# Moving sums of weights between three stages of a hybrid transformer block on one core

## The chip, the cores and the metric

The kernel runs on one core of one Trainium2 chip. The metric is the device time of one execution in microseconds (us). Three runs of the kernel before took 3123.35, 3115.73 and 3134.21 us, median 3123.35 us. Names of engines: PE is TensorE, PEld its weight loads, DVE is VectorE, ACT is ScalarE, POOL is GpSimd, SP is SyncE, which here issues nearly all DMAs.

## What is computed

One layer over 2064 tokens (16 learned meta tokens and 2048 inputs) with 1024 features. An input projection feeds three mixers (a linear recurrence, an attention with forgetting, and a delta-rule recurrence), an output projection joins them, and a feed-forward block follows:

```python
h = concat([meta, x])
p = rms_norm(h, g_mix_pre) @ w_in            # 1024 -> 3080 columns, three groups
mixed = concat([rg_lru(p), fox_attention(p), rwkv7(p)]) @ w_out
h = h + rms_norm(mixed, g_mix_post)
f = causal_dwconv3(rms_norm(h, g_ffn_pre) @ ffn_up)   # 1024 -> 2 * 2816
gate, val = split(f)
f = (gelu(gate) * val) @ ffn_down            # 2816 -> 1024
out = (h + rms_norm(f, g_ffn_post))[16:]
```

All numbers are float32. Every large product is made of three matmuls on operands that are split into a high part and the rest (`mm3`, lines 148 to 152). The split is a copy on ACT (L1528, rounded to the matmul's format) and a subtraction (L1529) on DVE or POOL.

## The kernel before

**Stages.** The input projection runs in three parts over the tokens (`w_in_part`), one unit for each 128 columns of `w_in`; each unit loads 512 KB of weights (`raw`, L143), splits them (L144, L145) and multiplies. From the first part on, the recurrences are woven in between its units. Then come the attention, the output projection, the first feed-forward product (`ffn_up`), and the second (`Down`).

**Seven products for eight.** Both feed-forward products are blocked two by two and use seven products, so some operands are sums of blocks of weights. For the first weights and a column block j of 128, the four raw blocks are `g0`, `g1` (gate, upper and lower half of the rows) and `v0`, `v1` (value); the sums are `s1 = v0 + v1`, `s2 = s1 - g0`, `s4 = g1 - s2`, `s3 = g0 - v0`, each 128x512 numbers. For the second weights, a pair k of row blocks gives four sums `t1` to `t4` in the same way, also 128x512 each.

**`ffn_up`.** There are 66 units: three blocks of tokens (`sup` 0 to 2), in each 22 column blocks j. A unit is seven products of 12 matmuls. While a unit's products run, the next unit's seven weight operands are made by an `UpWeights` object: a raw tile `uq` is loaded (L1587) into a ring of 10 buffers (`RAWS`), and split into a tile `uw` of a ring of 10. In block 0 of tokens every unit is "own": its four raw blocks are loaded, POOL computes the four sums (L1601), SP stores them to the scratch `scr_us` (L1602). In blocks 1 and 2 the unit is not own: it loads three raw blocks and four kept sums, seven loads. `POOLED` says which of the seven operands' subtractions L1529 run on POOL and not on DVE: one (operand 6) in an own unit, two (3 and 6) in another. At its end each unit multiplies gate and value on POOL (L1646, twice) and stores the result (L1647).

**`between`.** Between the units of a block, the next block's tokens are normalised and transposed (`ffn_norm`, L1489 and L1490) and their sums made on POOL (L1523).

**`weight_sums`.** The sums of the second weights, for ten pairs k: a load of 1 MB (L1550), four POOL operations (L1547), a store of 1 MB to `scr_ds` (L1559), through one tile `ds`. The code asks for them beside the units of parts 1 and 2 of the input projection. A scheduler at build time sets the order of each engine's instructions, and nothing ties these to a place: it puts them in the first part, at 25 to 195 us.

Each engine, and SP's queue of DMA issues, runs its instructions in the order of the program, so one that waits holds those behind it.

Of the kernel before, what the change touches and what calls it, by code (L numbers as in the profile page):

```python
# [8 lines left out]
F32 = mybir.dt.float32  # L9
# [4 lines left out]
ALU = mybir.AluOpType  # L14
# [4 lines left out]
P = 128  # L19
# [9 lines left out]
FF = 2816  # L29
NFF = FF // P  # L30


class Core:


    def __init__(self, tc, ctx):
        self.tc = tc
        self.nc = tc.nc
        self.ctx = ctx
        self.uid = 0  # L40
# [98 lines left out]
def load_parts(core, raws, src, hi, lo):  # L139

    pool, tag, bufs = raws
    raw = pool.tile(list(hi.shape), F32, tag=tag, name=core.n("raw"), bufs=bufs)
    core.nc.sync.dma_start(raw[:], src)  # L143
    core.nc.scalar.activation(hi, raw[:], AF.Copy)  # L144
    core.nc.vector.tensor_tensor(lo, raw[:], hi, op=ALU.subtract)  # L145

# [247 lines left out]
class Attn:  # L394
# [1071 lines left out]
HK = KD // 2  # L1466
# [74 lines left out]
SUMS = ("s2", "s4", "s3", "s1")  # L1541


def weight_sums(core, pool, w_down, scr):

    nc = core.nc
    sub = lambda o, x, y: nc.gpsimd.tensor_tensor(o, x, y, op=ALU.subtract)  # L1547
    for k in range(DOWN_PAIRS):
        t = pool.tile([P, 4, 512], F32, tag="us", name=core.n("ds"))
        nc.sync.dma_start(  # L1550
            t[:].rearrange("p (i h) c -> p i (h c)", h=2),
            w_down[2 * P * k : 2 * P * (k + 1), :].rearrange("(i p) c -> p i c", p=P),
        )
        l0, r0, l1, r1 = (t[:, i] for i in range(4))
        sub(l0, r0, l0)
        sub(r0, r1, r0)
        sub(r1, r1, l0)
        sub(l1, l1, r1)
        nc.sync.dma_start(scr["ds"][k], t[:].rearrange("p s c -> p (s c)"))  # L1559
        yield  # L1560

# [6 lines left out]
class UpWeights:  # L1568
# [2 lines left out]

    def __init__(self, core, raws, ring, w_up, scr, j, sup):
        self.core, self.raws, self.ring, self.w_up, self.scr, self.j = core, raws, ring, w_up, scr, j
        self.own = sup == 0
        self.raw = {s: self.load(s) for s in ("g0", "v0", "v1", "g1")} if self.own else {}

    def new(self):
# [30 lines left out]
        return t  # L1608

POOLED = (3, 6), (6,)

# [277 lines left out]
def hybrid_block_kernel(ctx: ExitStack, tc: tile.TileContext, args, out):  # L1891
    a = {s: v[0] if s != "meta_tokens" else v for s, v in args.items()}
    nc = tc.nc
    core = Core(tc, ctx)
    scr = scratch(tc, ctx, core)
    x, meta = a["x"], a["meta_tokens"]
# [20 lines left out]
    with ExitStack() as p1:  # L1917
        core.const = pool(p1, "const1", 1)
        dp = pool(p1, "dp", 2, space=DRAM)
        rec = ExitStack()  # L1920
        ps_rw = pool(rec, "ps_rw", 2, space=PSUM, **right)
        ps_ae = pool(rec, "ps_ae", 1, space=PSUM, **right)
        gp = pool(rec, "gp", 1, **right)
        rp = pool(rec, "rp", 1, **right)
        with ExitStack() as p1a:
            ps_mm = pool(p1a, "ps_mm", 5, space=PSUM)
            g_pre = spread(pool(p1a, "gpre", 1), a["norm_mix_pre"], "g_pre")
            pools = {"xn": pool(p1a, "xn", 1), "nt": pool(p1a, "nt", 4), "w": pool(p1a, "w", 2), "st": pool(p1a, "st", 2)}
            sums = weight_sums(core, pool(p1a, "us", 1), a["ffn_down"], scr)
            following = w_in_norm(core, pools, ps_mm, x, meta, g_pre, 0)  # L1930
            for part in range(3):
                blocks = following
                if part == 0:
                    zeros = pools["st"].tile([P, PAD], F32, tag="sth", name="zeros")
                    nc.vector.memset(zeros[:], 0.0)
                    for r in range(0, A_ROWS + C_ROWS, P):
                        nc.gpsimd.dma_start(scr["p"][r : r + P, 0:PAD], zeros[:])
                units = w_in_part(core, pools, ps_mm, a["w_in"], blocks, scr)
                for _ in range(READY if part == 0 else 0):
                    next(units)  # L1940
                if part == 0:
# [28 lines left out]
        beside.finish()  # L1970
        for _ in R.ending:
            pass
        rec.close()
        p2 = ExitStack()
        ps_wo = [pool(p2, "ps_wo", 2, space=PSUM, **right)]
        with ExitStack() as p1b:
            more = pool(p1b, "ps_more", 1, space=PSUM, **right, **early)
            at = Attn(core, pool(p1b, "ap", 2, **early), pool(p1b, "ps_at", 1, space=PSUM), more, scr)
            at.run()
    qp = pool(ctx, "qp", 1, **early)  # L1980
    with ExitStack() as p3:
# [3 lines left out]
        tmp = pool(p3, "tmp", RAWS, **early)  # L1985
# [8 lines left out]
        with p2:  # L1994
# [7 lines left out]
            for i, (f, rows) in enumerate(FFN_TILES):  # L2002
# [5 lines left out]
                if i >= LATE and todo:  # L2008
                    q, f, rows = todo.pop(0)
# [8 lines left out]
        sums, ws, down = [iter(())], [], []  # L2018

        def between(sup, j):  # L2020

            sup += 1
            if j == 1 and sup < SUPERS:
                quarters[sup] = ffn_quarters(core, qp, sup)
                todo[:] = tiles[sup]
            elif j == 1:
                kept = qp.tile([P, DOWN_KEPT, 2, 512], F32R, tag="q", name=core.n("qd"))
                down.extend(kept[:, i] for i in range(DOWN_KEPT))
            elif sup == SUPERS:
                if j == DOWN_FROM:  # L2030
                    raw = lambda: tmp.tile([P, 512], F32, tag="uq", name=core.n("raw"))[:]
                    ws.append(down_operands(core, raw, lambda: down.pop(0), a["ffn_down"], scr, 0))
            elif todo:
                q, f, rows = todo.pop(0)
                ffn_norm(core, np_, ps_n, scr, f, rows, rs[q], g_fpre, quarters[sup], sup)
                if not todo:
                    sums.append(ffn_sums(core, quarters[sup], lambda: tc.issue_after(core.pooled.ins)))
            else:
                for _ in range(2):
                    next(sums[-1], None)  # L2040

        ffn_up(
            core, tmp, uw, up, ps_f, a["ffn_up"], cw, scr, between,
            lambda sup, i: ffn_operand(core, xo, quarters[sup], i),
        )
# [73 lines left out]
```

## Time and profile before

| what | value |
|---|---|
| median of three runs | 3123.35 us |
| the profiled execution's own time | 3122.89 us |
| its span | 3121.2 us |
| granted TensorE clock, mean of the span | 0.962 |
| busy: PE, PEld, DVE, ACT, POOL | 2925.9, 2492.2, 2251.1, 1452.4, 1301.9 us |
| moved by DMA | 443.72 MB, mean 142 GB/s |
| POOL, sums of the second weights (L1547) | 40 instructions, 58.3 us |
| POOL, sums of the first weights (L1601) | 88 instructions, 128.3 us |

A group's row reads: line, engine, operation, out<-in, shapes, count, then busy time, mean ns of one, and the idle time of the engine ahead of it with what ended it. "psu" are the accumulators of the first feed-forward product, "psp" those of the input projection, "rwraw" and "rwitmp" tiles of the recurrences.

### The profile page before, as it was taken

To read this page: it belongs to the slowest core of one execution; us is meant where nothing else is said; L and a number is where in the kernel's file an instruction comes from. 1 tells how busy PE (TensorE), PEld (TensorE's weight loads), DVE (VectorE), ACT (ScalarE), POOL (GpSimd) and SP (SyncE) were. 2 spreads that over 40 slices of the span, in tenths; PEclk is the share of its full clock that TensorE was granted. 3 is DMA by queue.
4 is the path that set the end of the run, shared out by engine and by line. 5 is a ranking of instruction groups with operands and counts; after the bars stand their busy time and mean duration, and the time that the engine had idled before them with its cause. 6 is when DMAs were issued, how large, how long until landed. Compare 5 with 4: busy or idle time off the path is not lost. (4 is left out here: it accounts for less than half of the span.)

```text
span 3121.2 us, 52484 instructions
## 1 busy us (share of the span) xinstructions
PE 2925.9 (94%) x18488; PEld 2492.2 (80%) x18488; DVE 2251.1 (72%) x4585; ACT 1452.4 (47%) x2716; POOL 1301.9 (42%) x1436
## 2 busy tenths in 40 slices
PE   6988999999978999999998899999999999999998
PEld 6987998999855664665576899899999999787776
DVE  6247655676688778877758898888778787547777
ACT  4135334344544444445533555566666665324332
POOL 3310001101134365446733568743533334547665
PEclk9999999999988788999999899999999999999999
DMA  6664333353353235544236555565665565535454
GB/s 205 226 204 137 101 97 100 107 140 104 97 143 81 64 84 142 130 117 107 65 107 201 162 171 158 167 193 170 166 166 166 166 188 162 174 105 167 143 161 142
DMA packets 456503, 443.72 MB, mean 142 GB/s; under 512 B 82496, under 2 KB 373514, under 8 KB 453408
## 3 DMA queue, kind: packets, MB, share of 16 engines
q1 hardware_dynamic: 455856, 439.99, 48.3%
q8 instruction: 145, 2.38, 0.3%
q14 instruction: 118, 0.97, 0.1%
q0 software_dynamic: 384, 0.39, 0.0%
HBM read 314.39 MB, written 125.87 MB: 141 GB/s over the span
## 5 line engine op out<-in xcount | busy, mean ns | idle before, releaser
L150 PE MATMUL psu<-xo,uw 128*128 128x344 f32 x1848 | 594.9, 326 | 25.2 <-DVE vb L1684 10.4
L151 PE MATMUL psu<-xo,uw 128*128 128x344 f32 x1848 | 597.1, 323 | 0.7 <-DVE xo L1529 0.7
L152 PE MATMUL psu<-xo,uw 128*128 128x344 f32 x1848 | 586.5, 322 | 0.0
L150 PE MATMUL psp<-xh,wh 128*128 128x384 f32 (+2 forms) x1152 | 382.0, 332 | 0.0
L152 PE MATMUL psp<-xh,wl 128*128 128x384 f32 (+2 forms) x1152 | 379.1, 330 | 3.0 <-DVE wl L145 3.0
L151 PE MATMUL psp<-xl,wh 128*128 128x384 f32 (+2 forms) x1152 | 378.2, 328 | 0.0
L150 PEld LDWEIGHTS psu<-xo,uw 128*128 128x128 f32 x1848 | 350.3, 190 | 31.4 <-DVE vb L1684 12.4
L1529 DVE TENSOR_TENSOR uw<-uq,uw 128x512 fp32r<-128x512 f32 x352 | 327.5, 935 | 59.5 <-ACT uw L1528 55.8
L151 PEld LDWEIGHTS psu<-xo,uw 128*128 128x128 f32 x1848 | 351.7, 190 | 1.1 <-DVE xo L1529 1.1
L152 PEld LDWEIGHTS psu<-xo,uw 128*128 128x128 f32 x1848 | 350.0, 190 | 0.0
L1528 ACT ACTIVATE uw<-uq 128x512 fp32r<-128x512 f32 x462 | 286.9, 627 | 102.8 <-PE psu L152 48.8
L640 ACT ACTIVATE p<-sc,bias 128x512 f32<-128x512 f32 (+4 forms) x352 | 197.6, 590 | 217.3 <-PE sc L636 181.8
L1640 DVE SCALAR_TENSOR_TENSOR uy<-psu,ffn_cols,uy 128x342 f32<-128x342 f32 (+1 forms) x396 | 224.0, 567 | 72.0 <-ACT uy L1638 70.9
L679 POOL TENSOR_TENSOR acc<-acc,p 128x512 f32<-128x512 f32 (+3 forms) x208 | 230.5, 1111 | 78.7 <-DVE acc L679 37.9
L1646 POOL TENSOR_TENSOR uy<-uy,uy 128x342 f32<-128x342 f32 (+1 forms) x132 | 146.3, 1109 | 224.5 <-DVE uy L1640 79.2
L152 PEld LDWEIGHTS psp<-xh,wl 128*128 128x128 f32 x1152 | 220.1, 191 | 10.3 <-issue 5.5
L150 PEld LDWEIGHTS psp<-xh,wh 128*128 128x128 f32 x1152 | 219.9, 191 | 7.1 <-issue 4.7
L151 PEld LDWEIGHTS psp<-xl,wh 128*128 128x128 f32 x1152 | 220.0, 191 | 6.4 <-issue 4.1
L1529 POOL TENSOR_TENSOR uw<-uq,uw 128x512 fp32r<-128x512 f32 x110 | 155.9, 1417 | 164.2 <-ACT uw L1528 137.8
L512 DVE TENSOR_REDUCE mc<-mx 128x1 f32<-128x400 f32 (+5 forms) x320 | 171.5, 554 | 55.3 <-PE mx L509 53.9
L1529 DVE TENSOR_TENSOR fo<-u,fo 128x896 fp32r<-128x896 f32 x88 | 104.4, 1187 | 118.6 <-ACT fo L1528 118.6
L1528 ACT ACTIVATE fo<-u 128x896 fp32r<-128x896 f32 x88 | 81.0, 922 | 230.9 <-POOL u L1756 120.9
(451 smaller groups left out, 6612.6 us busy)
## 6 DMA issues: line engine op xcount, KB each, us to landing
uq<-in_ffn_up_dram SPq DMA_DIRECT2D x220, 256.0 KB
uq<-scr_us SPq DMA_DIRECT2D x176, 256.0 KB
raw<-in_w_in_dram SPq DMA_DIRECT2D x72, 512.0 KB
scr_us<-uq SPq DMA_DIRECT2D x88, 256.0 KB
u<-scr_ff SPq DMA_DIRECT2D x88, 256.0 KB
scr_ff<-uy SPq DMA_DIRECT2D x110, 171.0 KB
q<-scr_qh SPq DMA_DIRECT2D x96, 128.0 KB
ds<-in_ffn_down_dram SPq DMA_DIRECT2D x10, 1024.0 KB
```

Source lines behind the costliest of these rows:

```text
L150: nc.tensor.matmul(out, ah, bh, start=first, stop=False, skip_group_check=more)
L151: nc.tensor.matmul(out, ah, bl, start=False, stop=False, skip_group_check=more)
L152: nc.tensor.matmul(out, al, bh, start=False, stop=last, skip_group_check=more)
L512: self.reduced = nc.vector.tensor_reduce(mc[:rows, i, ci : ci + 1], ps[:rows, :full], axis=AX.X, op=ALU.max)
L640: last = nc.scalar.activation(p[:rows, :w], ps[:rows, :w], AF.Exp, bias=bias[:rows, j : j + 1])
L679: eng.tensor_tensor(a, ps_[0][0][:rows, c0:n] if start and i == 1 else a, p[:rows, : n - c0], op=ALU.add)
L1528: core.nc.scalar.activation(hi, src, AF.Copy)
L1529: (eng or core.nc.vector).tensor_tensor(lo, src, hi, op=ALU.subtract)
L1640: stt(y[:, :n], src[:, i : n + i], cw[:, 44 * i + cc : 44 * i + cc + 1], y[:, :n], op0=ALU.mult, op1=ALU.add)
L1646: core.pooled = nc.gpsimd.tensor_tensor(v[:, :n], g[:, :n], v[:, :n], op=ALU.mult)
```

## The change

Three places get the sums. `weight_sums` goes. `up_sums` makes the sums of the first weights for the eleven odd column blocks (`EARLY`) beside the units of parts 1 and 2 of the input projection, one block after every fourth unit, through the tile that held `ds`. Its instructions on SP are ordered behind the latest load of `raw` by `issue_after`, which adds an order edge to a named instruction on the same engine. In block 0 of tokens the odd units are then no longer own: they load three raw blocks and four kept sums, and have two subtractions on POOL. The even units compute beside use as before. `down_sums` makes the sums of the second weights in blocks 1 and 2 of `ffn_up`: 40 POOL operations, one per unit and two after every fourth, each ordered behind the latest end of a unit (`core.pooled`), with four buffers of the ring of `uq` for each of ten pairs.

```diff
+def up_sums(core, pool, w_up, scr, js):
+    tt = nc.gpsimd.tensor_tensor
+    for j in js:
+        t = pool.tile([P, 4, HK, P], F32, tag="us", name=core.n("us"))
+        for u in range(2):
+            c0 = FF * u + P * j
+            nc.sync.dma_start(
+                t[:, 2 * u : 2 * u + 2].rearrange("p h k c -> p (h k) c"),
+                w_up[:, c0 : c0 + P].rearrange("(k p) c -> p k c", p=P),
+            )
+        g0, g1, v0, v1 = (t[:, i] for i in range(4))
+        tt(v1, v0, v1, op=ALU.add)
+        for o, x, y in ((v0, g0, v0), (g0, v1, g0), (g1, g1, g0)):
+            tt(o, x, y, op=ALU.subtract)
+        nc.sync.dma_start(scr["us"][j], t[:].rearrange("p s k c -> p (s k c)"))
+        yield
+def down_sums(core, raws, w_down, scr, after):
     for k in range(DOWN_PAIRS):
+        l0, r0, l1, r1 = q = [raws.tile([P, 512], F32, tag="uq", name=core.n("ds")) for _ in range(4)]
+        for i, t in enumerate(q):
+            at = P * (2 * k + i // 2)
+            nc.sync.dma_start(t[:], w_down[at : at + P, 512 * (i % 2) : 512 * (i % 2) + 512])
+        for i, (o, x, y) in enumerate(((l0, r0, l0), (r0, r1, r0), (r1, r1, l0), (l1, l1, r1))):
+            with after():
+                nc.gpsimd.tensor_tensor(o[:], x[:], y[:], op=ALU.subtract)
+            yield
+        for i, t in enumerate(q):
+            nc.sync.dma_start(scr["ds"][k, :, 512 * i : 512 * i + 512], t[:])
...
-        self.own = sup == 0
+        self.own = sup == 0 and j not in EARLY
...
+EARLY = range(1, NFF, 2)
...
-                    if part and i % 3:
-                        next(sums, None)
+                    if part and i % 4 == 0:
+                        with tc.issue_after(core.loaded.ins):
+                            next(sums, None)
...
+            for _ in range(1 + (j % 4 == 3) if sup else 0):
+                next(later, None)
```

The scheduler's order shows where this lands. First SP's queue in the first part of the input projection; `raw` are weights of `w_in`, `stp` results on their way to the scratch, `rwraw` the recurrences' reads of that scratch. Before:

```order
L1550 DMA ds_4076<-in_ffn_down_dram 128x2x1024
L209 DMA scr_p<-stp_798 128x400
L209 DMA scr_p<-stp_826 128x384
L143 DMA raw_1289<-in_w_in_dram 128x8x128
L209 DMA scr_p<-stp_860 128x400
L1559 DMA scr_ds<-ds_4076 128x2048
L209 DMA scr_p<-stp_888 128x384
L1550 DMA ds_4375<-in_ffn_down_dram 128x2x1024
L143 DMA raw_1384<-in_w_in_dram 128x8x128
```

The same place of the changed kernel:

```order
L209 DMA scr_p<-stp_798 128x400
L209 DMA scr_p<-stp_826 128x384
L143 DMA raw_1289<-in_w_in_dram 128x8x128
L209 DMA scr_p<-stp_860 128x400
L209 DMA scr_p<-stp_888 128x384
L143 DMA raw_1384<-in_w_in_dram 128x8x128
```

The loads and stores of `ds` are gone from between the loads of `raw`; the rest stands in the same order.

Second, POOL at the start of part 1, between two chains of a recurrence (`rwitmp`, L1101, which alternates with DVE). Before:

```order
L1101 TENSOR_TENSOR rwitmp_1972<-rwix_1969,rwia_1941 128x120
L1101 TENSOR_TENSOR rwitmp_1972<-rwix_1969,rwia_1941 128x128
L983 TENSOR_SCALAR rwe_2230<-rwe_2230 128x512
L1101 TENSOR_TENSOR rwitmp_2515<-rwix_2512,rwia_2484 128x16
L1101 TENSOR_TENSOR rwitmp_2515<-rwix_2512,rwia_2484 128x24
```

And in the changed kernel:

```order
L1101 TENSOR_TENSOR rwitmp_1972<-rwix_1969,rwia_1941 128x128
L983 TENSOR_SCALAR rwe_2230<-rwe_2230 128x512
L1557 TENSOR_TENSOR us_3520<-us_3520 128x512
L1559 TENSOR_TENSOR us_3520<-us_3520 128x512 x3
L1557 TENSOR_TENSOR us_4049<-us_4049 128x512
L1559 TENSOR_TENSOR us_4049<-us_4049 128x512 x3
L1101 TENSOR_TENSOR rwitmp_2515<-rwix_2512,rwia_2484 128x16
L1101 TENSOR_TENSOR rwitmp_2515<-rwix_2512,rwia_2484 128x24
```

Eight operations on `us`, which wait for loads, now stand ahead of the second chain; the tiles `us_5449` and `us_7812` are further ones right ahead of such a chain or inside it.

Third, POOL in block 0 of tokens of `ffn_up`; `uq` sums, `uy` ends of units, `q` sums of tokens, `uw` subtractions. Two units before:

```order
L1601 TENSOR_TENSOR uq_20229<-uq_20192,uq_20194 128x512
L1601 TENSOR_TENSOR uq_20192<-uq_20190,uq_20192 128x512
L1646 TENSOR_TENSOR uy_19979<-uy_19956,uy_19979 128x342
L1601 TENSOR_TENSOR uq_20249<-uq_20229,uq_20190 128x512
L1601 TENSOR_TENSOR uq_20269<-uq_20196,uq_20249 128x512
L1646 TENSOR_TENSOR uy_20022<-uy_20000,uy_20022 128x342
L1523 TENSOR_TENSOR q_18029<-q_18029 128x344 x2
L1529 TENSOR_TENSOR uw_20179<-uq_20034,uw_20179 128x512
L1601 TENSOR_TENSOR uq_20389<-uq_20352,uq_20354 128x512
L1601 TENSOR_TENSOR uq_20352<-uq_20350,uq_20352 128x512
L1646 TENSOR_TENSOR uy_20139<-uy_20116,uy_20139 128x342
```

And in the changed kernel, from one group of sums to the next:

```order
L1619 TENSOR_TENSOR uq_20407<-uq_20334,uq_20387 128x512
L1666 TENSOR_TENSOR uy_20165<-uy_20143,uy_20165 128x342
L1523 TENSOR_TENSOR q_18042<-q_18042 128x344
L1529 TENSOR_TENSOR uw_20317<-uq_20315,uw_20317 128x512
L1523 TENSOR_TENSOR q_18042<-q_18042 128x344
L1666 TENSOR_TENSOR uy_20273<-uy_20250,uy_20273 128x342
L1666 TENSOR_TENSOR uy_20320<-uy_20296,uy_20320 128x342
L1523 TENSOR_TENSOR q_18042<-q_18042 128x344 x2
L1529 TENSOR_TENSOR uw_20477<-uq_20332,uw_20477 128x512
L1619 TENSOR_TENSOR uq_20678<-uq_20641,uq_20643 128x512
```

Between two groups of four sums POOL now has a whole unit without any.

More of the change, by code (lines that the diff above doesn't have):

```diff
@@ L142, in load_parts @@
     raw = pool.tile(list(hi.shape), F32, tag=tag, name=core.n("raw"), bufs=bufs)
-    core.nc.sync.dma_start(raw[:], src)
+    core.loaded = core.nc.sync.dma_start(raw[:], src)
     core.nc.scalar.activation(hi, raw[:], AF.Copy)
@@ L1541 @@
 SUMS = ("s2", "s4", "s3", "s1")
-def weight_sums(core, pool, w_down, scr):
+def up_sums(core, pool, w_up, scr, js):
     nc = core.nc
-    sub = lambda o, x, y: nc.gpsimd.tensor_tensor(o, x, y, op=ALU.subtract)
-    for k in range(DOWN_PAIRS):
[L1549 to L1560, printed above, removed]
+    tt = nc.gpsimd.tensor_tensor
[14 more added lines that the diff above has]
+def down_sums(core, raws, w_down, scr, after):
+    nc = core.nc
+    for k in range(DOWN_PAIRS):
+        l0, r0, l1, r1 = q = [raws.tile([P, 512], F32, tag="uq", name=core.n("ds")) for _ in range(4)]
[8 more added lines that the diff above has]
+            nc.sync.dma_start(scr["ds"][k, :, 512 * i : 512 * i + 512], t[:])
 SUM_OF = {"s1": ("v0", "v1", ALU.add), "s2": ("s1", "g0", ALU.subtract), "s4": ("g1", "s2", ALU.subtract),
@@ L1928, in hybrid_block_kernel @@
             pools = {"xn": pool(p1a, "xn", 1), "nt": pool(p1a, "nt", 4), "w": pool(p1a, "w", 2), "st": pool(p1a, "st", 2)}
-            sums = weight_sums(core, pool(p1a, "us", 1), a["ffn_down"], scr)
+            sums = up_sums(core, pool(p1a, "us", 1), a["ffn_up"], scr, EARLY)
             following = w_in_norm(core, pools, ps_mm, x, meta, g_pre, 0)
@@ L2040, in between @@
                     next(sums[-1], None)
+        later = down_sums(core, tmp, a["ffn_down"], scr, lambda: tc.issue_after(core.pooled.ins))
         ffn_up(
```

## Prediction

> **What bounds the kernel now.** I read the page first, then the busy times by stage, then what PE waited for inside the stages that the change touches.
>
> ```profile
> span 3121.2 us, 52484 instructions
> PE 2925.9 (94%) x18488; PEld 2492.2 (80%) x18488; DVE 2251.1 (72%) x4585; ACT 1452.4 (47%) x2716; POOL 1301.9 (42%) x1436
> ```
>
> ```profile
> core 0: us, PE busy (x) PEld busy (x) DVE busy (x) ACT busy (x) POOL busy (x), PEclk, DMA share, GB/s
> 0.00:335.00 335.00, 284.51 (x1536) 269.60 (x1537) 178.75 (x441) 124.66 (x219) 77.24 (x87) 0.95 0.60 188
> 335.00:880.00 545.00, 533.43 (x5011) 482.72 (x5009) 350.73 (x805) 230.47 (x415) 56.03 (x100) 0.98 0.38 107
> 1720.00:2054.00 334.00, 314.41 (x1907) 309.39 (x1908) 288.71 (x398) 191.97 (x374) 229.94 (x162) 0.96 0.54 170
> 2054.00:2645.00 591.00, 589.27 (x3733) 587.61 (x3732) 458.85 (x735) 367.85 (x729) 234.18 (x209) 1.00 0.60 170
> ```
>
> The rows are the first part of the input projection, its parts 1 and 2, block 0 of tokens of the first feed-forward product, and its blocks 1 and 2. PE is the bound nearly everywhere: it idles 1.7 of 591 us in the last row and 11.6 of 545 us in the second. There is something to win only where it waits: in the first part (50 us, much of it the start) and in block 0 (20 us, and more at a lower clock). The change takes work from exactly these two and puts it into the two full ones.
>
> **Part A: the second weights' sums leave the first part.** PE's waits between 40 and 200 us, then who held whom:
>
> ```profile
> PE eps L388 <- DVE ccol L380: 7.8, 2, 7.2
> PE psp L152 <- DVE wl L145: 3.0, 1, 3.0
> ```
>
> ```profile
> 162.06 0.38 SPq L1550 DMA_DIRECT2D ds<-in_ffn_down_dram  x1
> 166.32 0.37 SPq L942 DMA_DIRECT2D rwraw<-scr_p  x1
> 169.42 0.55 ACT L1386 ACTIVATE rwe<-rwraw 128x416 f32<-128x416 f32 x1 [14.45 <-DMA rwraw<-scr_p]
> 151.28 0.56 DVE L57 COPY stp<-psp 128x384 f32<-128x384 f32 x1 [11.67 <-DMA scr_p<-stp]
> ```
>
> ```profile
> 155.00:160.00 5.00, 5.00 (x30) 5.00 (x29) 1.23 (x1) 0.00 (x0) 2.29 (x2) 1.00 0.38 138
> 175.00:180.00 5.00, 5.00 (x19) 4.99 (x18) 3.29 (x7) 3.55 (x8) 0.21 (x1) 0.55 0.82 301
> ```
>
> DVE waited 11.67 us for a store of `stp` to land, and PE then 3.0 us for `wl`. ACT waited 14.45 us for a read of `rwraw`, which SP issued only at 166.32, behind a load of 1 MB of `ds`; PE waited 7.2 us at the end of that chain. The last row shows what follows: the clock at 0.55, with 19 matmuls in 5 us where 30 had run, so 11 x 5.00/30 = 1.8 us more. Together 3.0 + 7.2 + 1.8 = 12.0 us, or 1.2 us for each of ten pairs. In the changed kernel SP's queue has no `ds` here. What is late next is the weights' own split, which keeps pace from 40 to 140 us. I take the whole, A = -12. Its ends are 0 (the read waits for its own stores whatever else moves) and -14 (some of the start too).
>
> [...]
>
> **Part B: eleven blocks of the first weights' sums enter parts 1 and 2.** Each is two loads of 512 KB, four POOL operations, a store of 1 MB. Their price on POOL and its waits are those of the sums that stood in the first part (40 to 200 us), and what they land beside is the recurrences' chain (335 to 880 us):
>
> ```profile
> L1547 POOL TENSOR_TENSOR ds<-ds 128x512 f32<-128x512 f32 x36 | 53.2, 1478 | 97.3 <-DMA ds<-in_ffn_down_dram 87.3 <-issue 7.9
> SPq L1559 <- POOL ds L1547: 30.5, 7, 6.7
> L1101 POOL TENSOR_TENSOR rwitmp<-rwix,rwia 128x16 f32<-128x16 f32 (+14 forms) x75 | 38.5, 514 | 159.7 <-DVE rwia L1096 99.1 <-DVE rwix L1102 35.1 <-DVE rs L89 23.8
> ```
>
> POOL gets 44 x 1.478 = 65 us on top of 56 in 545, which is nothing as a share. The traffic rises by 11 x 2 MB or 23 MB / 545 us = 42 GB/s, from 107 to about 149, below the 188 of the first part. What counts is order. On SP the store waits for POOL, and behind it stand stores of `stp`, the next load of `raw` and reads of `rwraw`; the sums before held SP 30.5 us in this way, while four buffers of `raw` kept PE fed. On POOL the four sums wait for their load, and behind them stand the chain L1101 and two scalings; DVE alternates with that chain and PE's recurrence products wait for DVE. The cover is POOL's idle time: it waited 99.1 us for DVE ahead of the chains, so a sum of 10.8 us of waiting (97.3 / 9) and 5.9 us of work mostly falls into it. If the first part's price carried over, it would be 11 x 1.2 = 13 us; if all hides, 0. The traffic is nearer to the quiet side and a sum comes only every fourth unit, so I take B = +5.
>
> **Part C: block 0 of tokens loses half of the sums made beside use.** The copies `ga` mark units 0, 22, 44 and 65:
>
> ```profile
> 1729.99 0.43 ACT L1673 ACTIVATE ga<-psu 128x344 f32<-128x344 f32 x1
> 2053.80 0.47 ACT L1673 ACTIVATE ga<-psu 128x344 f32<-128x344 f32 x1
> 2351.80 0.44 ACT L1673 ACTIVATE ga<-psu 128x344 f32<-128x344 f32 x1
> 2629.97 0.46 ACT L1673 ACTIVATE ga<-psu 128x344 f32<-128x344 f32 x1 [0.34 <-PE psu L152]
> ```
>
> Block 0 takes 323.8 / 22 = 14.72 us a unit, block 1 with the same norms and sums of tokens but kept weights 298.0 / 22 = 13.55, block 2 with neither 278.2 / 21 = 13.25. So 22 x 1.17 = 25.8 us hang on the sums beside use. The groups and waits of block 0 (1720 to 2054) show how:
>
> ```profile
> L1601 POOL TENSOR_TENSOR uq<-uq,uq 128x512 f32<-128x512 f32 x80 | 118.1, 1478 | 88.8 <-DMA uq<-in_ffn_up_dram 58.3 <-DVE uy L1640 13.0 <-DVE uw L1529 12.4
> L1646 POOL TENSOR_TENSOR uy<-uy,uy 128x342 f32<-128x342 f32 x42 | 56.5, 1345 | 8.9 <-DMA uq<-in_ffn_up_dram 4.5 <-ACT xo L1528 3.2 <-ACT uw L1528 1.2
> L1529 POOL TENSOR_TENSOR uw<-uq,uw 128x512 fp32r<-128x512 f32 x24 | 38.1, 1586 | 34.7 <-ACT uw L1528 34.7
> L1529 DVE TENSOR_TENSOR uw<-uq,uw 128x512 fp32r<-128x512 f32 x133 | 139.5, 1057 | 17.6 <-ACT uw L1528 16.6
> ```
>
> ```profile
> SPq L1602 <- POOL uq L1601: 138.8, 75, 6.2
> SPq L1587 <- POOL uw L1529: 31.4, 20, 4.0
> PE psu L150 <- DVE vb L1684: 9.1, 5, 3.2
> ```
>
> It is a loop: SP holds the next loads behind a store that waits for POOL (138.8 us), POOL then waits for those loads (58.3), and the ends of units queue behind. Over two units POOL works 8 x 1.478 + 4 x 1.345 + 2 x 1.586 = 20.4 us and about 5 of token sums in 29.4. After the change four sums go (-5.9) and one subtraction comes from DVE (+1.6): about 21 of the 26.5 that PE needs, with one wait for loads instead of two. DVE is relieved of that subtraction (1.06). If only odd units reach 13.55, C = -12.9; if all do, -25.8. The loop is cut once in each turn, so an even unit starts with a load issued a unit ahead: I take the middle, C = -19. Nothing here makes it slower, so the other end is 0.
>
> **Part D: the second weights' sums enter blocks 1 and 2.** 40 x 1.478 = 59 us raise POOL from 234 to 293 of 591. On SP ten groups of four loads wait for buffers of the ring, and behind them stand the loads of the next weights; on POOL the sums stand ahead of subtractions and ends of units. With four of ten buffers held, a load still runs six operands ahead, 6 x 13.55 / 7 = 11.6 us, twice the longest wait for a load that POOL had in block 0:
>
> ```profile
> POOL uq L1601 <- DMA uq<-in_ffn_up_dram: 58.3, 14, 5.9
> ```
>
> So most hides. The ends are 0 and the first part's price, 10 x 1.2 = 12; I take +3, since PE is full here and each slip would show.
>
> **Sum.** -12 + 5 - 19 + 3 = -23 against this execution's own 3122.89 us, which lies 0.5 us under the median of the runs: 3100 us. The scheduler also reorders what the change does not name, attention and recurrences among it; for that I allow what the three runs differ by, some 8 us.
>
> **Rivals.** *The first part's waits stay* (A = 0): the read of `rwraw` needs stores of `stp`, and these may land as late without `ds`. For it: SP held the read for 4 us. Against: the traffic then was 301 GB/s. 3122.9 + 5 - 19 + 3 = 3112 us.
>
> *Only odd units gain* (C = -13): each even unit still loads, adds and stores in turn. 3106 us.
>
> *POOL's waiting sums stall the recurrences, slower.* Three of the eleven stand right ahead of or inside a chain L1101. If loads come late, each holds it for 10.8 + 5.9 = 16.7 us, and PE behind it, with 1.8 us of clock: 3 x 18.5 = 56 us for B. -12 + 56 - 19 + 3 = +28, 3151 us. It turns the sign beyond half a per cent once B exceeds 44 us, so all three must be nearly wholly exposed. POOL's 99.1 us of idle time ahead of the chains speaks against.
>
> *Shared access of POOL and DVE.* Two neighbouring rows show the same subtraction on DVE without and with POOL at work:
>
> ```profile
> 1795.17 0.68 DVE L1529 TENSOR_TENSOR uw<-uq,uw 128x512 fp32r<-128x512 f32 x1
> 1799.66 1.41 DVE L1529 TENSOR_TENSOR uw<-uq,uw 128x512 fp32r<-128x512 f32 x1
> ```
>
> If every new sum in blocks 1 and 2 hits one such operation, DVE gains 40 x 0.73 = 29 us on 459 of 591. Where the norms already fill DVE this reaches PE, perhaps half: D = +15, 3112 us. [...]
>
> That the change doesn't do what it says is excluded by the scheduler's order.
>
> **Chances.** Forecast 0.50, first part's waits 0.17, odd units only 0.13, stalled recurrences 0.12, shared access 0.08. Half a per cent (15.6 us) is about what a measurement of this kernel can tell from no change. Faster than 3107.7 us: the forecast and half of the odd-units case, 0.57. Within: the other half, first part's waits and shared access, 0.31. Slower: 0.12. Low end: -14 + 0 - 26 + 0 = -40 gives 3083, with some of the 8 us 3078. High end: A = 0 with C = -13, B and D at 13 and 12 gives +12, 3135; I cut it at 3130, since all four together are unlikely, and leave the stalled recurrences out.
>
> **What would show it.** Right: no wait of PE over 2 us at 140 to 180 us; units 0 to 22 of the feed-forward product in about 305 us; SP's wait for POOL's sums halved; PE idle under 5 us in blocks 1 and 2; PE idle in parts 1 and 2 of the input projection up by no more than 5 us. Wrong: PE waits for `rwxu` behind POOL in parts 1 and 2, or block 0 unchanged at 14.7 us a unit.

## The result, and the profile after

The changed kernel takes 3091.09 us, median of four runs (3088.73 to 3094.16), beside 3122.85 us (3115.73 to 3134.21) for the kernel before: a ratio of 0.9888, 95% interval 0.9857 to 0.992. That is 31.8 us less, where 23 had been forecast (3100 us); it lies inside the range. The profiled execution took 3089.22 us, 33.7 us less than the one profiled before.

The head of its page, and busy times by stage. The first two stretches are those of the prediction; the last two are block 0 and blocks 1 and 2, which begin earlier now.

```profile
span 3087.5 us, 52530 instructions
PE 2920.0 (95%) x18488; PEld 2490.5 (81%) x18488; DVE 2230.6 (72%) x4574; ACT 1458.1 (47%) x2716; POOL 1320.6 (43%) x1447
```

```profile
0.00:335.00 335.00, 298.34 (x1643) 282.02 (x1644) 184.71 (x462) 130.36 (x226) 32.53 (x55) 0.97 0.48 143
335.00:880.00 545.00, 524.26 (x4953) 470.79 (x4951) 375.23 (x844) 231.24 (x418) 109.72 (x137) 0.97 0.51 145
1714.00:2015.00 301.00, 295.90 (x1869) 294.38 (x1868) 250.48 (x374) 185.19 (x363) 175.86 (x132) 0.99 0.59 176
2015.00:2597.00 582.00, 578.79 (x3657) 577.89 (x3656) 450.20 (x715) 358.32 (x711) 293.87 (x236) 0.99 0.68 203
```

In the first 335 us PE runs 107 matmuls more than before (1643 for 1536). The second row isn't the same work as before, since every stage has moved forward by some 19 us and the attention begins inside it. Block 0 loses only 5.1 us of PE's time, where it was 20, and blocks 1 and 2 lose 3.2, where it was 1.7.

To compare like with like I cut both traces at the same piece of work. The first cut is the 1153rd row of the products psp<-xh,wh / xl,wh / xh,wl, with which the second third of them begins (24 of 72 units); the second is the last such product; then come the copies `ga` of units 0, 22, 44 and 65. PE's rows at the first two cuts before, and after, then the copies after:

```profile
317.98 0.34 PE L150 MATMUL psp<-xh,wh 128*128 128x384 f32 x1
868.98 0.28 PE L152 MATMUL psp<-xh,wl 128*128 128x256 f32 x1
```

```profile
298.55 0.34 PE L150 MATMUL psp<-xh,wh 128*128 128x384 f32 x1
849.96 0.28 PE L152 MATMUL psp<-xh,wl 128*128 128x256 f32 x1
```

```profile
1714.51 0.44 ACT L1693 ACTIVATE ga<-psu 128x344 f32<-128x344 f32 x1
2015.02 0.45 ACT L1693 ACTIVATE ga<-psu 128x344 f32<-128x344 f32 x1
2318.30 0.47 ACT L1693 ACTIVATE ga<-psu 128x344 f32<-128x344 f32 x1
2597.04 0.46 ACT L1693 ACTIVATE ga<-psu 128x344 f32<-128x344 f32 x1 [0.33 <-PE psu L152]
```

All profiles of this study, cut in this way (us; the twelve experiments are told below):

| kernel | first 24 units | parts 1, 2 | to block 0 | block 0 | block 1 | block 2 | rest |
|---|---|---|---|---|---|---|---|
| before | 318.0 | 551.0 | 861.0 | 323.8 | 298.0 | 278.2 | 491.2 |
| after | 298.6 | 551.4 | 864.6 | 300.5 | 303.3 | 278.7 | 490.5 |
| e1 down only | 299.1 | 548.6 | 862.0 | 323.2 | 300.1 | 279.4 | 493.0 |
| e2 up only | 316.9 | 573.1 | 876.0 | 303.9 | 297.5 | 278.2 | 493.5 |
| e3 down sums in parts 1, 2 | 300.2 | 563.8 | 867.9 | 324.3 | 297.2 | 278.2 | 494.6 |
| e4 stores on ACT | 316.5 | 547.3 | 868.7 | 322.4 | 297.7 | 278.2 | 491.7 |
| e9 without s3 | 315.0 | 547.9 | 867.2 | 314.3 | 298.0 | 278.2 | 491.9 |
| e7 first eleven early | 299.0 | 552.5 | 859.3 | 302.0 | 303.2 | 278.7 | 491.4 |
| e6 all early | 302.1 | 602.6 | 858.2 | 295.3 | 302.8 | 278.4 | 491.0 |
| e5 down in block 2 | 298.9 | 551.8 | 864.7 | 303.4 | 297.5 | 287.5 | 489.4 |
| e12 down behind norms | 299.5 | 551.8 | 870.7 | 302.7 | 297.5 | 280.6 | 492.6 |
| e13 both | 298.2 | 560.9 | 862.0 | 301.6 | 297.4 | 283.5 | 491.4 |
| e14 no stores | 303.0 | 550.9 | 861.7 | 324.2 | 300.4 | 278.4 | 490.4 |
| e15 loads only | 301.0 | 548.5 | 868.9 | 324.7 | 300.4 | 278.4 | 492.1 |

Down a column one sees how far a stage repeats where its work is the same: block 0 with all its sums, its program untouched, within 1.5 us (before, e1, e3, e14, e15), block 1 with no new sums beside its norms within 0.8 (before, e2 to e4, e9, e5, e12, e13), but the stretch from the projection to block 0 only within 13, e2's 876.0 apart (before and e4 do the same work there in nearly the same order, and take 861.0 and 868.7). So the prices are read from the columns, and small ones not from whole times.

Between the two profiles the stages moved by -19.4, +0.4, +3.5, -23.3, +5.3, +0.6 and -0.8: -33.7. The prediction had -12, +5, nothing, -19 and +3 for the two blocks.

### The profile page after: what moved, and what is told of

The parts are those of the page before. It is cut to its first block, busy times and chain, and to the rows that moved or that the text cites. A ratio compares the mean times of both kernels' runs of the same rounds, so it can differ in the third digit from the quotient of the medians.

```text
span 3087.5 us, 52530 instructions
## 1 busy us (share of the span) xinstructions
PE 2920.0 (95%) x18488; PEld 2490.5 (81%) x18488; DVE 2230.6 (72%) x4574; ACT 1458.1 (47%) x2716; POOL 1320.6 (43%) x1447
## 5 line engine op out<-in xcount | busy, mean ns | idle before, releaser
L150 PE MATMUL psu<-xo,uw 128*128 128x344 f32 x1848 | 590.1, 324 | 14.9 <-DVE wx L1457 4.8
L1529 DVE TENSOR_TENSOR uw<-uq,uw 128x512 fp32r<-128x512 f32 x341 | 313.6, 926 | 62.4 <-ACT uw L1528 59.2
L1666 POOL TENSOR_TENSOR uy<-uy,uy 128x342 f32<-128x342 f32 (+1 forms) x132 | 141.9, 1075 | 270.5 <-DVE uy L1660 78.9
L1529 POOL TENSOR_TENSOR uw<-uq,uw 128x512 fp32r<-128x512 f32 x121 | 175.6, 1451 | 140.6 <-ACT uw L1528 115.9
```

Source lines behind the costliest of these rows:

```text
L150: nc.tensor.matmul(out, ah, bh, start=first, stop=False, skip_group_check=more)
L1529: (eng or core.nc.vector).tensor_tensor(lo, src, hi, op=ALU.subtract)
L1666: core.pooled = nc.gpsimd.tensor_tensor(v[:, :n], g[:, :n], v[:, :n], op=ALU.mult)
```

## The experiments

**e1, e2: one half of the change at a time.** e1 keeps `down_sums` and lets every unit of block 0 be own; e2 keeps `up_sums` and leaves the second weights' sums where they were.

```diff
e1:  -self.own = sup == 0 and j not in EARLY
     +self.own = sup == 0
     -sums = up_sums(...)   (and its four lines in the loop over the parts)
e2:  -later = down_sums(...)   (and its two lines in between)
     +def weight_sums(...): as before, its tile from "us"
     +us = pool(p1a, "us", 1)
     +downs = weight_sums(core, us, a["ffn_down"], scr)
     -if part and i % 4 == 0:
     +if part and i % 3:
     +    next(downs, None)
     +if part == 2 and i % 2 == 0:
          (the sums of the first weights, as in the changed kernel)
```

> Only the second weights' sums move (out of the input projection, into blocks 1 and 2); in block 0 every unit still makes its own sums. Theory (each part of the change has its own price): the first part ends its 24 units 19 us earlier, as in the changed kernel (298.6 for 318.0), block 0 stays at 324 us, block 1 takes 5 us more than before; together 3123 - 19 + 5 = 3109 us (3104 to 3114). Rival (the first part's waits did not come from these sums but went with the whole program's new order): the 24 units end at 318 again and the time is 3123 + 5 = 3128 us.

> Only the first weights' sums of the odd units move (into part 2 of the input projection); the second weights' sums stay in its first part, in the places of before. Theory: the first part ends its 24 units at 318 as before, block 0 takes 301 us for 324, block 1 298 as before; 3123 - 23 + 0 to 4 for the eleven sums in part 2 = 3100 to 3104 us. Rival (block 0 gained by what came before it, not by its own fewer sums): block 0 stays over 315 us and the time over 3114.

e1: ratio to the kernel before 0.9958 (95% interval 0.9937 to 0.9979; the brackets below are such intervals too), 13 us less. Its first 24 units end at 299.1, and block 0 stays at 323.2; the rival falls. e2: 1.0051 (1.0033 to 1.0069), a little slower, by 16 us. The copies of units 0 and 22 in e1, and in e2:

```profile
1709.76 0.43 ACT L1693 ACTIVATE ga<-psu 128x344 f32<-128x344 f32 x1
2033.00 0.47 ACT L1693 ACTIVATE ga<-psu 128x344 f32<-128x344 f32 x1
```

```profile
1766.02 0.43 ACT L1712 ACTIVATE ga<-psu 128x344 f32<-128x344 f32 x1
2069.88 0.44 ACT L1712 ACTIVATE ga<-psu 128x344 f32<-128x344 f32 x1
```

Block 0 gains its 20 us in e2 as expected (303.9), with the first part left as it was. So the two gains are separate, and each comes with its own edit. But e2 as a whole missed by some 40 us: with all eleven sums in part 2, one every second unit, that part took 26 us more. Part 2 (from the 2306th product of psp to the last) before, and in e2:

```profile
640.26:868.98 228.72, 226.56 (x2360) 205.65 (x2359) 155.38 (x360) 106.04 (x193) 21.45 (x40) 0.99 0.39 107
```

```profile
635.10:890.00 254.90, 240.58 (x2359) 217.18 (x2359) 183.97 (x369) 105.19 (x194) 81.60 (x84) 0.93 0.63 187
```

The matmuls are as many. PE idles 14.3 us for 2.2, and the other 14 us are busy time at a granted clock of 0.93 for 0.99. The stretch behind it, to block 0, took 876.0 us, more than in any other run.

**e6: all 22 blocks early.** `EARLY = range(NFF)`, a sum every second unit (`i % 2 == 0`).

> The changed kernel with all 22 units' sums made in parts 1 and 2 of the input projection, a sum every second unit there in place of every fourth. Theory (the price in parts 1 and 2 grows with how dense the sums stand, as when eleven of them stood in part 2 alone, where that part took 26 us more and what follows 8 to 15 more): parts 1 and 2 take 40 to 55 us more than in the changed kernel, block 0 falls from 300.5 to 298, and the whole is 3135 to 3160 us. Rival (the price is by number, 0.4 us a sum): parts 1 and 2 take 4 us more, the whole is 3090 to 3096 us.

Measured 1.0015 (0.9995 to 1.0035), no faster than the kernel before. Its two parts:

```profile
302.09:646.55 344.46, 325.83 (x2695) 295.41 (x2695) 215.44 (x449) 132.83 (x235) 92.33 (x100) 0.96 0.55 164
646.55:904.74 258.19, 244.71 (x2411) 218.33 (x2410) 179.57 (x374) 102.44 (x187) 79.01 (x80) 0.93 0.58 174
```

Eleven sums in each part, and each part is some 25 us dearer than in the changed kernel: parts 1 and 2 take 51 us more (602.6 for 551.4), as the theory of density had it (its 3135 to 3160 us for the whole lie above the measured 3132.7, in part since block 0 fell to 295.3 and not to 298). Block 0 therefore had 28.5 us to give in all, and the changed kernel took 23.3 of them with half of the sums.

**e3: is it the place or the pair?** The kernel before with its ten pairs held to parts 1 and 2.

```diff
-core.nc.sync.dma_start(raw[:], src)
+core.loaded = core.nc.sync.dma_start(raw[:], src)
...
-    if part and i % 3:
-        next(sums, None)
+    if part and i % 4 == 0:
+        with tc.issue_after(core.loaded.ins):
+            next(sums, None)
```

> The kernel before, with the second weights' sums still in the input projection and still in one tile of 1 MB, but held to parts 1 and 2 by the same device that the change uses for its sums. Theory (the place makes the price: the first part is short of transfers, parts 1 and 2 are not): the 24 units end 19 us earlier, parts 1 and 2 take 0 to 3 us more, 3123 - 19 + 2 = 3106 us (3102 to 3110). Rival (a pair costs 1.2 to 1.9 us of waiting wherever SP and POOL have it in their queues): parts 1 and 2 give back 12 to 19 us, 3116 to 3123 us.

Measured 0.9991 (0.9972 to 1.0009): nothing gained. The first part gave its 18 us, and parts 1 and 2 took 12.8 back (563.8 for 551.0); the stretch behind them took 6.9 more, which is no more than it moves by between runs. The rival's figure holds here. Eleven of the first weights' sums at the same spacing cost about 3 (after, e5, e7 and e12 take 551.4 to 552.5; before, e1, e4, e9, e14 and e15, which have none there, 547.3 to 551.0), though e13, with as many, took 560.9. Why ten pairs in one load of 1 MB each cost more than eleven blocks in two loads of 512 KB is not settled.

**e4, e9, e7: what sets the pace of block 0.** Three edits of block 0 alone: the stores of the own sums issued by ACT; the sum s3 left out; the first eleven units early in place of every second one (the first two edit the kernel before, the last the changed kernel).

```diff
e4:  -core.nc.sync.dma_start(self.kept(s), raw[:])
     +core.nc.scalar.dma_start(self.kept(s), raw[:])
e9:  +if s != "s3":
         core.nc.gpsimd.tensor_tensor(raw[:], self.raw[x][:], self.raw[y][:], op=op)
e7:  -EARLY = range(1, NFF, 2)
     +EARLY = range(NFF // 2)
```

> The kernel before, with the stores of block 0's own sums issued by ACT, which waits for the same sum right behind to split it, and no longer by SP. The sums are all there. Theory A (the loop over SP: loads held behind a store that waits for POOL): block 0 falls from 324 to 300 to 308 us, 3099 to 3107 us in all. Theory B (POOL's own time for four sums a unit makes the pace): block 0 stays at 318 to 324 us, 3117 to 3123 us; anything between divides the gain.

> The kernel before, without the operation that makes the sum s3 in block 0 (22 POOL operations left out, a quarter of the sums there; its halves are stored and used as loaded). Loads, stores, buffers and queues are those of before. Theory A (POOL's own time sets block 0's pace: 1.48 us less a unit for POOL): block 0 falls from 324 to 300 to 308 us, the whole to 3100 to 3107. Theory B (the turn of loads and stores sets it, with the same loads to wait for): block 0 stays over 316 us, the whole over 3115.

> The changed kernel with the first eleven units' sums made early in place of every second unit's; as many sums, as many loads. Theory A (alternation: a unit with kept weights lets POOL catch up before the next that makes its own): units 0 to 10 run at 13.6 and 11 to 21 at 14.55 as they did before, block 0 takes 310 us for 300.5, the whole 3100 us. Theory B (each sum that leaves block 0 is worth as much, by POOL's total time): block 0 takes 299 to 303 us, the whole 3090 to 3094 us.

e4: 1.0015 (0.9994 to 1.0036), block 0 at 322.4. What SP waited for in its block 0:

```profile
SPq L1647 <- POOL uy L1646: 165.0, 39, 9.9
```

```profile
L1601 POOL TENSOR_TENSOR uq<-uq,uq 128x512 f32<-128x512 f32 x80 | 120.7, 1511 | 84.2 <-DMA uq<-in_ffn_up_dram 45.8 <-DVE uy L1640 19.1 <-DVE uw L1529 14.9
```

SP no longer stands behind the stores of the sums (138.8 us before); it stands 165.0 us behind POOL at the next thing that POOL makes, the stores of `uy` (31.8 before). So the edit did not free SP as it was meant to: loads still stand behind a store that waits for POOL, and the run neither confirms nor clears the loop. It shows that moving these stores alone gains nothing, since POOL is as late for what SP waits for next.

e9: 0.9953 (0.9926 to 0.9981), block 0 at 314.3, under theory B's 316 and over theory A's 308. With every load, store and buffer left in place, 22 POOL operations are worth 9.5 us, 0.43 each; in the changed kernel 44, with their loads and stores, are worth 23.3, 0.53 each. The wait for loads did not shrink with them (58.3 us before):

```profile
L1602 POOL TENSOR_TENSOR uq<-uq,uq 128x512 f32<-128x512 f32 x60 | 89.5, 1491 | 112.2 <-DMA uq<-in_ffn_up_dram 62.2 <-DVE uw L1529 17.8 <-issue 14.9
```

So most of the price goes with the number of POOL's operations, and not with that wait. e7: 0.9862 (0.984 to 0.9885), block 0 at 302.0 where 310 was expected of alternation. Its copies of units 0, 11 and 22; then those of unit 11 in the changed kernel, in the kernel before and in e9:

```profile
1710.78 0.43 ACT L1693 ACTIVATE ga<-psu 128x344 f32<-128x344 f32 x1
1861.06 0.44 ACT L1693 ACTIVATE ga<-psu 128x344 f32<-128x344 f32 x1
2012.75 0.47 ACT L1693 ACTIVATE ga<-psu 128x344 f32<-128x344 f32 x1
```

```profile
1868.52 0.44 ACT L1693 ACTIVATE ga<-psu 128x344 f32<-128x344 f32 x1
1893.63 0.46 ACT L1673 ACTIVATE ga<-psu 128x344 f32<-128x344 f32 x1
1896.78 0.46 ACT L1674 ACTIVATE ga<-psu 128x344 f32<-128x344 f32 x1
```

150.3 and 151.7 us for the halves, where the changed kernel has 154.0 and 146.5. The sum is nearly the same: for the block as a whole it matters little which units lose their sums. But half a microsecond is a mean, and not the price of each operation. The kernel before has 163.6 and 160.2 us for its halves, e9 166.7 and 147.6: a quarter of the operations left every unit of e9, and the whole gain came in units 11 to 21. Units 11 to 21 of e7 still make all their sums and took 8.5 us less than before. Why a sum is dear in one unit and nearly free in another was not tried.

**e5, e12, e13: where the second weights' sums stand.** All in block 2, two a unit; or from unit 9 of block 1 on, behind its norms, at the changed kernel's pace; and the last together with e7's edit.

```diff
     -for _ in range(1 + (j % 4 == 3) if sup else 0):
e5:  +for _ in range(2 if sup == 2 else 0):
e12: +for _ in range(1 + (j % 4 == 3) if sup == 2 or sup and j > 8 else 0):
```

> The changed kernel with all forty sums of the second weights in block 2 (two a unit) and none in block 1. Theory (their price is one load of a norm that stands in SP's queue behind their stores, and norms are only in block 1): block 1 falls from 303.3 to 298 to 300 us, block 2 stays under 280.5; the whole is 3 to 5 us under the changed kernel, 3086 to 3089 us. Rival (each sum costs its 0.15 us wherever it stands, by the access it shares with DVE): block 1 298, block 2 284 to 285, the whole as the changed kernel, 3091 us.

> The changed kernel with the second weights' sums begun only at unit 9 of block 1, behind its norms, at the same pace as before (five sums in four units). Theory (their price in block 1 was a norm's load behind their stores, their price in block 2 at two a unit was the density): block 1 takes 298 to 300 us for 303.3, block 2 279 to 281, the whole 3 to 5 us under the changed kernel, 3086 to 3088 us. Rival (a price of 0.15 us for each sum wherever it stands): blocks 1 and 2 together stay at 582 us, the whole at 3091.

> The last one with the first eleven units' sums made early in place of every second unit's. If the two edits add: block 0 as it was with the first half early (302), blocks 1 and 2 as expected of the last one (578 to 580), the whole 3083 to 3087 us, under the changed kernel's 3091. If they don't, because units that make their own sums now run up to block 1: block 1 over 301 us and the whole 3088 to 3092.

The changed kernel pays for these sums at one place. The longest wait of PE in its block 1, with the rows around it of SP, DVE and POOL, then the busy times of the ten microseconds from 2080:

```profile
2066.12 2.98 POOL L1575 TENSOR_TENSOR ds<-ds,ds 128x512 f32<-128x512 f32 x2
2069.60 0.38 SPq L1578 DMA_DIRECT2D scr_ds<-ds  x1
2071.19 0.63 SPq L1489 DMA_DIRECT2D xt<-scr_h  x1
2078.29 1.28 DVE L1490 SCALAR_TENSOR_TENSOR xt<-xt,rsv,g_fpre 128x1024 f32<-128x1024 f32 x1 [5.22 <-DMA xt<-scr_h]
2082.07 0.65 PE L150 MATMUL psu<-xo,uw 128*128 128x344 f32 x1 [2.71 <-ACT u L1699]
```

```profile
2080.00:2085.00 5.00, 2.93 (x10) 2.93 (x11) 4.74 (x8) 2.04 (x5) 3.54 (x3) 0.64 0.43 115
2085.00:2090.00 5.00, 5.00 (x27) 4.94 (x26) 4.59 (x10) 4.41 (x9) 2.56 (x3) 0.68 0.71 219
```

A norm's load of `xt` was issued behind stores of sums, and its reader started 7.1 us later; DVE stood 5.22 us for it, PE 2.71, and PE's clock was 0.64 and 0.68 in the mean of the two rows. That unit took 18.8 us for 14.9. It recurs in e6 and e7 (19.3 and 18.3), but not in e1, which has the same sums there: 15.2 us for that unit, 300.1 for the block. So it is a meeting of one load with these stores, and not a price that the sums always have. Taking the sums out from among the norms does remove it: block 1 takes 297.5 in e5 and in e12, for 303.3. But e5 pays in block 2, 287.5 us, over both figures that had been expected; e12 pays 280.6 there, as expected. In block 2 of e5, two of SP's waits, and one of ACT's:

```profile
SPq L1572 <- DMA scr_ds<-ds: 24.7, 9, 4.2
SPq L1605 <- DMA scr_ds<-ds: 22.0, 12, 3.4
```

```profile
ACT uw L1528 <- DMA uq<-scr_us: 17.6, 10, 5.0
```

Two sums a unit hold the ring: loads, of sums and of weights (L1605), wait 46.7 us for stores that have not landed, and ACT waits for weights. The whole times are 0.9879 (0.9857 to 0.9902) for e5, 0.9881 (0.9857 to 0.9905) for e12, 0.9889 (0.9869 to 0.991) for e13, against 0.9888 for the changed kernel: none can be told from it. In e12 blocks 1 and 2 are 3.9 us shorter, and the stretch ahead of block 0 happened to be 6.1 longer; in e13 parts 1 and 2 were 9.5 longer and one unit of block 2 took 21.6 us for 13.5. Their medians, 3093.7 and 3096.1 us, lie over the 3086 to 3088 and 3083 to 3087 expected, but the kernel before took 3128.0 beside them where it took 3122.9 beside the changed kernel: the gain that was expected of them is neither shown nor ruled out. e7 has the lowest ratio of all, and its interval too overlaps with the changed kernel's.

**e14, e15: what in the first part cost.** e1 with loads and POOL operations of the ten pairs put back into the first part, without stores; then with the operations cut to a column.

```diff
 e1 +def weight_sums(...): as before, without its last dma_start
e15 -l0, r0, l1, r1 = (t[:, i] for i in range(4))
    +l0, r0, l1, r1 = (t[:, i, :1] for i in range(4))
```

> The kernel in which only the second weights' sums moved, and which ended the first part's 24 units at 299.1 us, with the ten loads of 1 MB and the forty POOL operations put back into the first part, but without their stores (the sums made there are not used). Theory A (SP held by stores that wait for POOL, 30.5 us in the kernel before): without stores the 24 units end at 299 to 303 us. Theory B (the loads of 1 MB in SP's queue ahead of the small reads, and their traffic): they end at 311 to 318.

> The same with the forty POOL operations cut to one column each, so that little more than the ten loads of 1 MB is left of the sums in the first part. Theory B (loads and traffic): the 24 units still end at 311 to 318 us. Theory C (POOL's time, 59 us in the first part, delays POOL's work for the recurrence): they end at 299 to 305 here and at 311 to 318 in the run with the full operations.

The 24 units ended at 303.0 and 301.0, so A's figure and not the 311 to 318 us of B or, for e14, of C; but the runs do not settle what A said. Without stores the pairs follow each other faster, and the last load now goes out before the place where the trouble was. The last two loads of e14; then what SP issued for the pairs, and one store of `stp`, in the kernel before from 140 us on, and its wait at the read of `rwraw`:

```profile
119.88 0.38 SPq L1570 DMA_DIRECT2D ds<-in_ffn_down_dram  x1
130.50 0.38 SPq L1570 DMA_DIRECT2D ds<-in_ffn_down_dram  x1
```

```profile
144.65 0.38 SPq L1550 DMA_DIRECT2D ds<-in_ffn_down_dram  x1
157.40 0.32 SPq L1559 DMA_DIRECT2D scr_ds<-ds  x1
158.25 1.16 SPq L209 DMA_DIRECT2D scr_p<-stp  x1
181.13 0.38 SPq L1550 DMA_DIRECT2D ds<-in_ffn_down_dram  x1
```

```profile
SPq L942 <- DMA scr_p<-stp: 3.8, 1, 3.8
```

What they do show is that the pairs beside the first twelve units cost nothing there at the pace of the kernel before, or a little faster. From the first to the 577th product of psp it takes 105.68 us before, after and in e14, though SP waited in e14 as long for POOL as before:

```profile
SPq L1570 <- POOL ds L1567: 32.9, 7, 6.7
```

Only the start came later in e14, the first product at 46.4 for 42.6 in e1. In e15, where the ten loads follow each other faster still (the last at 87.50 us, for 130.50), the same units took 110.2 us, 4.5 more. The rest of A's price falls where pairs stood at 140 to 195 us in the kernel before, beside the recurrences' first reads: there a store of `stp` was issued 0.85 us behind a store of 1 MB (158.25 behind 157.40), and the read at 166.32 waited 3.8 us for such a store to land, eight microseconds after that issue. No run kept pairs without stores at that place, so whether the queue or the traffic made that store slow stays open.

## Why the prediction was right, and where it was not

The mechanism held: two places gain and two pay, and no other moved by more than it does between runs. What was to show it does: no wait of PE at 140 to 180 us, block 0 in 300.5 us for the 305 forecast, PE idle 3.2 us in blocks 1 and 2 where under 5 was asked, and in parts 1 and 2, cut at the same work, 8.0 for 4.0. The sizes were off, and three steps of the reasoning were wrong. With the means of the columns over all kernels that share an edit (other densities, and stages that an experiment itself edits, left out), the four terms are -17.5 for the first part (299.1 for 316.6), +2.9 for parts 1 and 2 (551.9 for 549.0, e13 left out; +4.6 with it), -21.7 for block 0 (302.3 for 324.0) and +4.5 for blocks 1 and 2 (580.4 for 575.9): -31.8, beside the 31.8 us that the medians show. That these agree to the tenth is luck, since the stretch ahead of block 0 alone moves by more. The forecast of 23 was short by 9 us: A was too small by 5.5 to 7.4 and C by 2.7 to 4.3, B 2 too dear, and against these D too small by 1.5 to 2.9.

**A was under-sized, -12 for -17.5 to -19.4.** Units 12 to 14 gave 13.1 (31.7 to 18.6 us), against 12.0 from the two waits and the clock; that part was read well. Left out were the start (the first product at 42.0 for 44.7, put only into the end of the range) and a further 3.6 us in units 14 to 24, behind pairs that stood there until 195 us. The rival in which the first part's waits stay is out by e1. The step that failed is the division by ten: "1.2 us for each of ten pairs" is no price of a pair, since the pairs beside units 0 to 12 cost nothing and a few later ones most of it. The load ahead of the read was not told apart from the store ahead of it, and is not yet.

**B was about right, +5 for +3, and its upper end was reckoned the wrong way.** It was the first part's price times eleven, 13 us. The changed kernel's density stayed under it (e13, the dearest, paid 11.9), but the price does not go by the number: e2 and e6 paid some 25 us a part at twice the density. The rival that turns the sign, with 56 us for sums in the way of the recurrences, was thought to need three sums nearly wholly exposed; with the spacing halved B is over the 44 us that turn the sign (602.6 for 549.0 in e6), and it comes from many short waits and the clock (0.93), not from three long ones. PE does wait for the chains behind POOL in e2 (320 to 870 us), but for 4.0 us in all:

```profile
PE rps L1125 <- POOL rwitmp L1101: 4.0, 2, 2.9
```

Whether POOL's order, SP's, or 187 GB/s for 107 does most of it was not tried apart.

**C came out at -21.7 to -23.3 for -19, and not by alternation.** The argument was a loop that is cut once in each turn, with gains for odd units first; -19 was the middle of two limits, so that it came near is in part luck. e7 shows the same gain without alternation, e9 shows a gain without any load or store taken away and with POOL's wait for loads as long as before, and e4 that moving SP's store moves SP's wait. The block's time goes by how many operations POOL has, about half a microsecond for each in the mean, until the block is at 13.4 us a unit (295.3 / 22 in e6). "Only odd units gain" (-13) falls. Why an operation of POOL costs that is not shown. It can be POOL's own time, with or without the loop. It can also be DVE, which was busy 280.0 of the block's 323.8 us: its subtraction took 1057 ns in the mean before (in the prediction), 1000 in e9 and 973 here, and the change gave one of them in each odd unit to POOL. No run tells the two apart. DVE's row in the changed kernel:

```profile
L1529 DVE TENSOR_TENSOR uw<-uq,uw 128x512 fp32r<-128x512 f32 x120 | 115.7, 973 | 9.9 <-ACT uw L1528 9.1
```

POOL's groups in block 0 of the changed kernel:

```profile
L1619 POOL TENSOR_TENSOR uq<-uq,uq 128x512 f32<-128x512 f32 x40 | 61.7, 1546 | 32.1 <-DMA uq<-in_ffn_up_dram 14.3 <-DVE uy L1660 9.8 <-DVE uw L1529 6.6
L1666 POOL TENSOR_TENSOR uy<-uy,uy 128x342 f32<-128x342 f32 x42 | 48.5, 1155 | 77.6 <-DVE uy L1660 35.5 <-ACT u L1699 27.9 <-ACT uw L1528 9.2
```

SP's wait for the sums was to be halved, and it is (138.8 to 71.6 us):

```profile
SPq L1620 <- POOL uq L1619: 71.6, 38, 5.2
```

Ahead of the ends of units (L1666) POOL now waits 77.6 us, most of it for DVE and ACT, where it had waited 8.9: POOL now runs ahead of its work.

**D was +3 for +4.5 to +5.9.** That loads run far enough ahead was true but for one: the norm's load, which is not one of the ring's, was not in the reckoning of what stands behind the sums in SP's queue. Some of the rival of shared access is there. In rows of one such subtraction alone, blocks 1 and 2 of the changed kernel have 72 beside an idle POOL, none over 0.69 us, and 39 beside a POOL that worked throughout, 0.98 us in the mean (0.69 and 0.99 before, with 95 and 16 rows). DVE's split of the weights in blocks 1 and 2, before and after:

```profile
L1529 DVE TENSOR_TENSOR uw<-uq,uw 128x512 fp32r<-128x512 f32 x215 | 185.2, 864 | 41.9 <-ACT uw L1528 39.2
```

```profile
L1529 DVE TENSOR_TENSOR uw<-uq,uw 128x512 fp32r<-128x512 f32 x215 | 192.8, 901 | 52.6 <-ACT uw L1528 50.1 <-DMA ds<-in_ffn_down_dram 0.2
```

It costs DVE 7.6 us where 29 had been reckoned at most, and PE little: in e12, where the forty sums begin behind the norms, block 1 is at its old 297.5, and block 2, with most of them, 2.4 us over.

## What to carry to other kernels

In this kernel side work has no price of its own: pairs beside one stretch cost nothing, those beside the next some 17 us, and twice as many sums to a stage cost many times as much (parts 1 and 2: 53.6 us in e6 for 2.9). Look for the place where such work meets a short transfer that a chain waits for, move it from there, and keep it thin. Where an engine is late, count its operations before moving a store: here moving the wait from one store to the next changed nothing, and a quarter of the operations less did. Cut both traces at the same work before reading a gain, since some stages here repeat to within one or two microseconds where whole runs differ by nearly twenty.

## What the runs showed of the hardware

In a wait of 2.71 us, the one at 2082.07 above, TensorE's granted clock fell to half. Three single microseconds of the changed kernel, one inside the wait and two behind it:

```profile
2081.00:2082.00 1.00, 0.00 (x0) 0.00 (x0) 1.00 (x3) 0.81 (x3) 1.00 (x2) 0.70 0.15 57
2087.00:2088.00 1.00, 1.00 (x7) 1.00 (x6) 1.00 (x2) 0.94 (x4) 0.56 (x1) 0.50 0.74 182
2088.00:2089.00 1.00, 1.00 (x7) 1.00 (x7) 1.00 (x3) 1.00 (x3) 0.00 (x0) 0.89 0.76 211
```

By such rows the granted clock was 0.50 from 2082 to 2088; with the means of 0.70 and 0.89 in the rows beside, half speed lasted some 6.8 us, 6.2 of them behind the wait. Matmuls of 128x344 started 0.29 us apart there (2082.52 to 2085.10), for 0.16 just ahead of the wait and again from 2088.24 on. So by the clock some 3.1 us were lost behind a wait of 2.71 (6.2 x 0.50, an estimate). Not each such wait does it: ahead of 1823.44 PE stood 2.56 us for `vb`, and the clock stayed at 1.00 in the wait and in the eight microseconds behind it. What tells the two apart was not tried. A learner here should count short waits too, and read what follows them from the clock.
